# A decoder trunk on one core: three instead of two of eight pairs of a W_up group with seven products, 2048-column splits, token sums made late in the group

## The chip, the cores and the metric

The kernel runs on one core of a Trainium2 chip. The metric is the device time of one execution in microseconds. Five engines have their own in-order instruction queues and meet at semaphores: TensorE (PE, with its weight loads PEld), VectorE (DVE), ScalarE (ACT), GpSimd (POOL, nearly unused here) and SyncE (SP), which issues the DMAs.

## The reference

Two decoder layers over 256 tokens of width 2048, in float32. A layer has attention (sliding window in layer 0, block-sparse in layer 1, which for 256 tokens is causal attention; both with four memory heads), an output projection, a norm, and an MLP of width 8192. The change touches the MLP:

```python
mix = jnp.concatenate([self_out, mem_out], axis=-1) @ w_o[layer]
h = layer_norm(ALPHA * h + mix, ln_g[layer, 0], ln_b[layer, 0])
ffn = jnp.square(jax.nn.relu(h @ w_up[layer])) @ w_down[layer]
h = layer_norm(ALPHA * h + ffn, ln_g[layer, 1], ln_b[layer, 1])
```

## The kernel before, in words

**Products.** Every float32 operand is split into a high part (`hi`, rounded to the matmul's format by ScalarE, L96) and a low part (`lo`, the rest, by VectorE, L97). A product of a 128-row block of activations with a 512-column block of weights is three matmuls (L254 to L256): hi by hi, hi by lo, lo by hi. Each of the three first needs its weights' `hi` or `lo`.

**The MLP's order.** A layer's MLP is four chunks of 2048 hidden columns. A chunk has two W_up groups of 1024 columns, called its first and second UP group, and then two W_down groups, its first and second DOWN group. In layer 1 the first UP group of the first chunk, and in both layers the second DOWN group of the last chunk, are made by another function (`aform`, two half groups). So `mlp_group` makes 8 + 7 UP groups and 7 + 7 DOWN groups.

**A group.** `mlp_group` takes 16 blocks of 128 rows as eight pairs, in the order `ORDER`. A pair's weights are one DMA of 1 MB. Six pairs are normal: eight products, 24 matmuls, into the four PSUM banks `ps_g` (two token halves by two column halves). Two pairs (`FAST`, at places 2 and 4 of the order, counted from 0) take seven products, 21 matmuls. For these VectorE makes sums of weight blocks (`t`, L116, L119, L120) and, once for a set of activations, sums of token blocks (`fast_acts`, lines 125 to 137, into `sum_h` or `sum_g`). Four of the seven products go to four more banks `P1`, `P5`, `P6`, `P7`, which `early` (L486 to L490 in UP groups, L502 to L512 in DOWN groups) adds up after the last seven-product pair. At a group's end four VectorE instructions (L639 in UP groups) add the banks `ps_g` to these sums, and the banks are free for the next group.

**Between the groups.** Hooks in a group's first two pairs transpose the group before (`transposed`, L426 to L429: TensorE, then ScalarE, then VectorE) into `gT`, the DOWN groups' activations. `fast_acts(gt[0], sum_g)` is called in the hook of the second UP group's second pair, after the third of four transposes.

**Buffers and queues.** `raw` has 4 buffers of 2048 columns: DMA targets, the weight sums `t`, and `fast_acts`' workspace `x_f` take them in turn. `whi` and `wlo` have 7 buffers each of 1024 columns. `ps_mm` (for `ps_g`) and `ps_at` (for the four `P` banks and the transposes) have 4 banks each. A scheduler that runs before the kernel moves instructions of an engine past each other where nothing depends on the order, from its own estimate of when operands are ready; the built order is fixed.

Of the kernel before, what the change touches and what calls it, by code (L numbers as in the profile page):

```python
# [74 lines left out]
def trunk(ctx: ExitStack, tc: tile.TileContext, a: dict, out: bass.AP):  # L75
# [48 lines left out]
    def fast_acts(x, s_):  # L124


        raw = wp.tile([P, 2048], F32, name="x_f", tag="raw", bufs=NRAW)
        f = raw[:, :1024].rearrange("p (k t) -> p k t", k=4)
        nc.vector.tensor_tensor(f, x[:, :, 0].bitcast(F32), x[:, :, 1].bitcast(F32), ALU.add)
        a11, a21 = f[:, 0:4:2, :P], f[:, 0:4:2, P:]  # L130
        a12, a22 = f[:, 1:4:2, :P], f[:, 1:4:2, P:]
        s = raw[:, 1024:].rearrange("p (q u t) -> p q u t", q=4, u=2)
        nc.vector.scalar_tensor_tensor(s[:, 0], a21, -1.0, a22, op0=ALU.mult, op1=ALU.subtract)
        nc.vector.scalar_tensor_tensor(s[:, 1], s[:, 0], -1.0, a11, op0=ALU.mult, op1=ALU.subtract)
        nc.vector.tensor_tensor(s[:, 2], a11, a21, ALU.subtract)
        nc.vector.tensor_tensor(s[:, 3], a12, s[:, 1], ALU.subtract)
        split(s_[:, 0], s_[:, 1], raw[:, 1024:])
# [442 lines left out]
    for l in range(LAYERS):  # L580
# [148 lines left out]
```

## Time and profile before

| | us |
|---|---|
| median of 3 runs | 2082.78 (2081.52 to 2083.8) |
| the profiled execution | 2085.73, of which the trace's span is 2083.6 |
| TensorE busy | 2023.7 (97%) |
| VectorE busy | 1540.2 (74%) |
| ScalarE busy | 1045.6 (50%) |
| mean granted TensorE clock | 0.984 of full speed |

The profile is one execution. Busy time of TensorE says that matmuls are under way, not at which clock: the granted clock stands beside it in the views by window. A timeline row gives the start, the duration, the instruction and, in brackets, how long its engine was idle before it and what ended that.

### The profile page before, as it was taken

What the parts mean: (1) busy time and instruction counts of PE and PEld (TensorE: products, weight loads), DVE (VectorE), ACT (ScalarE), POOL (GpSimd) and SP (SyncE); (2) the same over time, 40 slices, a digit from 0 to 9 for tenths busy, and PEclk for the clock granted to TensorE, in tenths of its full rate; (3) what the DMA queues carried; (4) which work ended last, traced back from release to release, by engine and by line L of the source; (5) the groups of instructions that cost most, each with busy time, mean ns of one, the idle gap of its engine ahead of it and who ended that gap; (6) DMA issues with size and microseconds to landing.
All of it is one profiled execution on the core that took longest, in us unless ns stands there. A gap on an engine that the chain in (4) does not pass through costs nothing.

```text
span 2083.6 us, 23980 instructions
## 1 busy us (share of the span) xinstructions
PE 2023.7 (97%) x9326; PEld 1675.4 (80%) x9326; DVE 1540.2 (74%) x1951; ACT 1045.6 (50%) x1351; POOL 1.2 (0%) x8
## 2 busy tenths in 40 slices
PE   9999999999999999999999999999999999999997
PEld 7888888788778878878888888778887887888786
DVE  6566669688597868768885665769786876877785
ACT  5555535554464455456444554346445544654551
POOL 0000000000000000000000000000000000000000
PEclk9999999999999999999999999999999999999999
DMA  9644545455356545445754445425654554564562
GB/s 330 255 143 160 202 162 203 160 204 181 142 208 220 197 157 205 175 146 219 271 222 171 153 162 202 142 103 211 221 194 161 203 177 146 214 219 173 205 220 81
DMA packets 56273, 391.63 MB, mean 188 GB/s; under 512 B 6368, under 2 KB 6368, under 8 KB 9696
## 3 DMA queue, kind: packets, MB, share of 16 engines
q1 hardware_dynamic: 56160, 390.10, 52.1%
q8 instruction: 73, 1.20, 0.2%
q14 instruction: 40, 0.33, 0.0%
HBM read 387.98 MB, written 2.10 MB: 187 GB/s over the span
## 4 chain that ended last, share of the span: by engine, by line
PE 92%; DVE 6%; ACT 1%; issue 0%; DMA 0%; SPq 0%; DVEq 0%; ACTq 0%
PE ps_g L256 17%; PE ps_g L255 17%; PE ps_g L254 17%; PE ps_w L189 7%; PE ps_a L211 5%; PE ps_a L212 5%; PE ps_a L213 5%; PE ps_w L191 4%; PE P L254 3%; PE P L256 3%; PE P L255 3%; PE pt_h L426 2%; PE ps_m L536 1%; PE ps_m L538 1%; PE ps_m L537 1%; DVE h L419 1%
## 5 line engine op out<-in xcount | busy, mean ns | idle before, releaser
L97 DVE TENSOR_TENSOR wlo<-raw,whi 128x1024 fp32r<-128x1024 f32 (+1 forms) x706 | 815.7, 1174 | 329.0 <-ACT whi L96 324.9
L96 ACT CAST whi<-raw 128x1024 fp32r<-128x1024 f32 (+1 forms) x706 | 693.5, 1014 | 596.3 <-PE ps_g L256 323.6
L255 PE MATMUL ps_g<-wlo,hT 128*128 128x512 f32 x780 | 305.8, 392 | 0.1
L256 PE MATMUL ps_g<-whi,hT 128*128 128x512 f32 x780 | 305.9, 392 | 0.0
L254 PE MATMUL ps_g<-whi,hT 128*128 128x512 f32 x780 | 302.6, 395 | 0.9 <-ACT whi L96 0.7
L254 PE MATMUL ps_g<-whi,gT 128*128 128x512 f32 x728 | 285.3, 393 | 0.0
L256 PE MATMUL ps_g<-whi,gT 128*128 128x512 f32 x728 | 283.5, 390 | 0.0
L255 PE MATMUL ps_g<-wlo,gT 128*128 128x512 f32 x728 | 283.4, 390 | 0.0
L96 ACT CAST whi<-t 128x1024 fp32r<-128x1024 f32 x116 | 122.0, 1052 | 120.9 <-PE ps_g L256 45.0
L254 PEld LDWEIGHTS ps_g<-whi,hT 128*128 128x128 f32 x780 | 147.8, 190 | 33.7 <-ACT whi L96 3.8
L255 PEld LDWEIGHTS ps_g<-wlo,hT 128*128 128x128 f32 x780 | 147.7, 189 | 31.3 <-DVE wlo L97 0.5
L256 PEld LDWEIGHTS ps_g<-whi,hT 128*128 128x128 f32 x780 | 147.6, 189 | 31.0
L97 DVE TENSOR_TENSOR wlo<-t,whi 128x1024 fp32r<-128x1024 f32 x116 | 141.6, 1223 | 41.2 <-ACT whi L96 40.9
L256 PEld LDWEIGHTS ps_g<-whi,gT 128*128 128x128 f32 x728 | 136.7, 188 | 28.8
L255 PEld LDWEIGHTS ps_g<-wlo,gT 128*128 128x128 f32 x728 | 136.8, 188 | 27.6
L254 PEld LDWEIGHTS ps_g<-whi,gT 128*128 128x128 f32 x728 | 136.6, 188 | 27.2
L189 PE MATMUL ps_w<-hT,whi 128*128 128x512 f32 x320 | 119.9, 414 | 0.0
L189 PE MATMUL ps_w<-xT,whi 128*128 128x512 f32 x320 | 119.9, 414 | 0.0
L211 PE MATMUL ps_a<-whi,ot 128*128 128x512 f32 x256 | 101.7, 397 | 0.0
L213 PE MATMUL ps_a<-whi,ot 128*128 128x512 f32 x256 | 99.8, 390 | 0.0
L212 PE MATMUL ps_a<-wlo,ot 128*128 128x512 f32 x256 | 99.7, 389 | 0.0
L429 DVE TENSOR_TENSOR gT<-pt_h,gT 128x512 fp32r<-128x512 f32 x64 | 43.9, 688 | 67.0 <-ACT gT L428 67.0
(184 smaller groups left out, 2910.1 us busy)
## 6 DMA issues: line engine op xcount, KB each, us to landing
raw<-in_wup_dram SPq DMA_DIRECT2D x120, 1024.0 KB, 4.9
raw<-in_wdn_dram SPq DMA_DIRECT2D x112, 1024.0 KB, 4.9
raw<-in_wo_dram SPq DMA_DIRECT2D x32, 1024.0 KB, 4.8
raw<-in_wq_dram SPq DMA_DIRECT2D x24, 1024.0 KB, 4.8
raw<-in_wdn_s_dram SPq DMA_DIRECT2D x16, 1024.0 KB, 4.9
raw<-in_wmk_dram SPq DMA_DIRECT2D x8, 1024.0 KB, 6.2
raw<-in_wv_dram SPq DMA_DIRECT2D x8, 1024.0 KB, 7.3
raw<-in_wk_dram SPq DMA_DIRECT2D x8, 1024.0 KB, 4.8
```

The costliest lines, as they stand in the source:

```text
L96: nc.scalar.copy(hi, src)
L97: nc.vector.tensor_tensor(lo, src, hi.bitcast(F32), ALU.subtract)
L189: nc.tensor.matmul(ps, hi[:, kk:kk + P], x.rearrange("p s t -> p (s t)"), start=(k == 0), stop=False)
L191: nc.tensor.matmul(ps[:, :T], lo[:, kk:kk + P], x[:, 0], start=False, stop=(k == KT - 1))
L211: nc.tensor.matmul(ps[t], xh, hi, start=st, stop=False)
L212: nc.tensor.matmul(ps[t], xh, lo, start=False, stop=False)
L213: nc.tensor.matmul(ps[t], xl, hi, start=False, stop=en)
L254: nc.tensor.matmul(bank, xh, hi, start=st, stop=False)
L255: nc.tensor.matmul(bank, xh, lo, start=False, stop=False)
L256: nc.tensor.matmul(bank, xl, hi, start=False, stop=en)
L426: nc.tensor.transpose(pt[:, k], src[:, k * P:(k + 1) * P], ident)
L429: nc.vector.tensor_tensor(xt[:, :, 1, t * P:(t + 1) * P], pt, hi.bitcast(F32), ALU.subtract)
```

## The change

The numbers of a group become arguments. UP groups use `UP`: the order (3, 4, 0, 5, 1, 6, 2, 7) with pairs 0, 1 and 2 as seven-product pairs, at places 2, 4 and 6; `early` now comes after place 6. DOWN groups use `DOWN`, the numbers of before.

Weights are split 2048 columns at a time (1536 and 2048 in a seven-product pair: B11, B22, B21 and then the four sums); `whi` and `wlo` have 4 buffers each of 2048 columns. So that the three unchanged blocks lie side by side, the host stores a pair's last two blocks in the other order.

`fast_acts` is a generator of two steps, one for the sums and one for their split. For `sum_h` (three pairs now) the steps are in hooks of the first UP group's places 0 and 1; for `sum_g` in hooks of the second UP group's places 5 and 6. The sums have no buffers of their own for `sum_g`: they use those of `v` and `mk` of the attention, and `sum_h` uses `pts` for its third pair.

```diff
-NHI = 7
+NHI = 4
...
-ORDER = (2, 3, 0, 4, 1, 5, 6, 7)
-FAST = (0, 1)
+
+UP = ((3, 4, 0, 5, 1, 6, 2, 7), 3)
+DOWN = ((2, 3, 0, 4, 1, 5, 6, 7), 2)
...
-        def pair(s, n):
-            hi = wp.tile([P, 1024], F32R, name="whi", tag="whi", bufs=NHI)
-            lo = wp.tile([P, 1024], F32R, name="wlo", tag="wlo", bufs=NHI)
+        def pairs(s, n):
+            hi = wp.tile([P, 2048], F32R, name="whi", tag="whi", bufs=NHI)
+            lo = wp.tile([P, 2048], F32R, name="wlo", tag="wlo", bufs=NHI)
             split(hi[:, :n], lo[:, :n], s)
...
-        pair(raw[:, :1024], 1024)
-        nc.vector.tensor_tensor(t_[:, 0:2], b[:, 0:2], b[:, 2:3].broadcast_to([P, 2, 512]), ALU.subtract)
-        pair(b[:, 3], 512)
-        pair(t_[:, 0:2].rearrange("p q c -> p (q c)"), 1024)
+        pairs(raw[:, :1536], 1536)
+        nc.vector.tensor_tensor(t_[:, 0:2], b[:, 0:2], b[:, 3:4].broadcast_to([P, 2, 512]), ALU.subtract)
         nc.vector.tensor_tensor(t_[:, 2], b[:, 1], t_[:, 0], ALU.add)
-        nc.vector.tensor_tensor(t_[:, 3], b[:, 3], t_[:, 2], ALU.subtract)
-        pair(t_[:, 2:4].rearrange("p q c -> p (q c)"), 1024)
+        nc.vector.tensor_tensor(t_[:, 3], b[:, 2], t_[:, 2], ALU.subtract)
+        pairs(t_.rearrange("p q c -> p (q c)"), 2048)
...
+    def fast_acts(xs, units):
...
+        for j in range(0, len(units), 2):
+            n = len(units[j:j + 2])
+            x = xs[j // 2][:, :2 * n]
+            raw = wp.tile([P, 2, 8, P], F32, name="x_f", tag="raw", bufs=NRAW)
...
+            nc.vector.tensor_tensor(f, x[:, :, 0].bitcast(F32), x[:, :, 1].bitcast(F32), ALU.add)
...
+            nc.vector.scalar_tensor_tensor(s[:, :, 0], a21, -1.0, a22, op0=ALU.mult, op1=ALU.subtract)
+            nc.vector.scalar_tensor_tensor(s[:, :, 1], s[:, :, 0], -1.0, a11, op0=ALU.mult, op1=ALU.subtract)
+            nc.vector.tensor_tensor(s[:, :, 2], a11, a21, ALU.subtract)
+            nc.vector.tensor_tensor(s[:, :, 3], a12, s[:, :, 1], ALU.subtract)
+            parts += [s[:, u] for u in range(n)]
+        yield
+        for (hi, lo), s in zip(units, parts):
+            split(hi, lo, s)
+        yield
...
     def weights(src, parts=1):
...
+        hi = wp.tile([P, 2048], F32R, name="whi", tag="whi", bufs=NHI)
+        lo = wp.tile([P, 2048], F32R, name="wlo", tag="wlo", bufs=NHI)
+        for c in range(0, 2048, n):
+            split(hi[:, c:c + n], lo[:, c:c + n], raw[:, c:c + n])
+        return [(hi[:, c:c + 1024], lo[:, c:c + 1024]) for c in (0, 1024)]
...
                     if sum_h is None:
-                        sum_h = ap_.tile([P, 2, 4, 2, P], F32R, name="sum_h", tag="sum_h")
-                        fast_acts(hT[0], sum_h)
+                        sum_h = sum_units(UP[1], ("sum_h0", "sum_h1", "pts"))
+                        steps = fast_acts(hT, sum_h)
+                        hooks[0, 0] = hooks[1, 1] = lambda s=steps: next(s)
+                    if v_ == 1:
+                        steps = fast_acts(gt, sum_g)
+                        hooks[5, 0] = hooks[6, 0] = lambda s=steps: next(s)
...
                     transposed(us[b], gt[2 * v_ + b % 2], b // 2, 0)
-                    if v_ == 0 and b == 2:
-                        fast_acts(gt[0], sum_g)
```

**Place one: VectorE, first part of layer 0's third chunk's second UP group.** Before, its queue has the first group's transposed tiles (`gT`), the token sums (`x_f`, `sum_g`) and only then the weights of the seven-product pair at place 2 (`raw_5964`):

```order
L429 TENSOR_TENSOR gT0_5528<-pt_h_5884,gT0_5528 128x4x128
L429 TENSOR_TENSOR gT1_5529<-pt_h_5907,gT1_5529 128x4x128
L429 TENSOR_TENSOR gT0_5528<-pt_h_5926,gT0_5528 128x4x128
L129 TENSOR_TENSOR x_f_5933<-gT0_5528 128x1024
L429 TENSOR_TENSOR gT1_5529<-pt_h_5947,gT1_5529 128x4x128
L133 SCALAR_TENSOR_TENSOR x_f_5933<-x_f_5933 128x256
L135 TENSOR_TENSOR x_f_5933<-x_f_5933 128x256
L134 SCALAR_TENSOR_TENSOR x_f_5933<-x_f_5933 128x256
L136 TENSOR_TENSOR x_f_5933<-x_f_5933 128x256
L97 TENSOR_TENSOR sum_g_5532<-x_f_5933,sum_g_5532 128x1024
L116 TENSOR_TENSOR t_5966<-raw_5964 128x1024
L97 TENSOR_TENSOR wlo_5968<-raw_5964,whi_5967 128x1024
```

Now, in the same place, that pair's weights (`raw_5431`) and even the sums for the pair at place 4 (`t_5498`) stand ahead of or among the transposed tiles:

```order
L98 TENSOR_TENSOR wlo_5435<-raw_5431,whi_5434 128x1536
L654 TENSOR_TENSOR u_n_5286<-u_n_5286,ps_g_5053 128x512
L654 TENSOR_TENSOR u_n_5287<-u_n_5287,ps_g_5054 128x512
L118 TENSOR_TENSOR t_5433<-raw_5431,t_5433 128x512
L119 TENSOR_TENSOR t_5433<-raw_5431,t_5433 128x512
L117 TENSOR_TENSOR t_5498<-raw_5496 128x1024
L440 TENSOR_TENSOR gT0_5045<-pt_h_5363,gT0_5045 128x4x128
L118 TENSOR_TENSOR t_5498<-raw_5496,t_5498 128x512
L119 TENSOR_TENSOR t_5498<-raw_5496,t_5498 128x512
L98 TENSOR_TENSOR wlo_5442<-t_5433,whi_5441 128x2048
L440 TENSOR_TENSOR gT1_5046<-pt_h_5382,gT1_5046 128x4x128
L440 TENSOR_TENSOR gT0_5045<-pt_h_5401,gT0_5045 128x4x128
```

The token sums are gone from this place; the first pair's `lo` of 1536 columns stands before the end of the group before.

**Place two: VectorE, the end of the first UP group of that chunk.** Before, the sums of `early` lie among splits of the group's last pairs and of the next group's place 0, and the four additions of `ps_g` follow each other:

```order
L97 TENSOR_TENSOR wlo_5813<-raw_5806,whi_5812 128x1024
L488 TENSOR_TENSOR u_n_5730<-u_n_5731,P5_5606 128x512
L97 TENSOR_TENSOR wlo_5859<-raw_5856,whi_5858 128x1024
L489 TENSOR_TENSOR u_n_5731<-u_n_5731,P7_5608 128x512
L490 TENSOR_TENSOR u_n_5732<-u_n_5731,P5_5606 128x512
L97 TENSOR_TENSOR wlo_5863<-raw_5856,whi_5862 128x1024
L97 TENSOR_TENSOR wlo_5900<-raw_5897,whi_5899 128x1024
L97 TENSOR_TENSOR wlo_5904<-raw_5897,whi_5903 128x1024
L639 TENSOR_TENSOR u_n_5729<-u_n_5729,ps_g_5533 128x512
L639 TENSOR_TENSOR u_n_5730<-u_n_5730,ps_g_5534 128x512
L639 TENSOR_TENSOR u_n_5731<-u_n_5731,ps_g_5535 128x512
L639 TENSOR_TENSOR u_n_5732<-u_n_5732,ps_g_5536 128x512
```

Now `early` starts after the splits of the group's last pair and the next group's first, and its sums, the additions of `ps_g` and the next group's splits (`raw_5376` is its place 1, `raw_5431` its place 2) alternate:

```order
L117 TENSOR_TENSOR t_5433<-raw_5431 128x1024
L98 TENSOR_TENSOR wlo_5342<-raw_5339,whi_5341 128x2048
L498 TENSOR_TENSOR u_n_5286<-u_n_5284,P6_5117 128x512
L98 TENSOR_TENSOR wlo_5379<-raw_5376,whi_5378 128x2048
L499 TENSOR_TENSOR u_n_5285<-u_n_5286,P5_5116 128x512
L654 TENSOR_TENSOR u_n_5284<-u_n_5284,ps_g_5051 128x512
L500 TENSOR_TENSOR u_n_5286<-u_n_5286,P7_5118 128x512
L654 TENSOR_TENSOR u_n_5285<-u_n_5285,ps_g_5052 128x512
L501 TENSOR_TENSOR u_n_5287<-u_n_5286,P5_5116 128x512
L98 TENSOR_TENSOR wlo_5435<-raw_5431,whi_5434 128x1536
L654 TENSOR_TENSOR u_n_5286<-u_n_5286,ps_g_5053 128x512
L654 TENSOR_TENSOR u_n_5287<-u_n_5287,ps_g_5054 128x512
```

What frees the banks `ps_g` has moved behind two splits for the next group.

**Place three: VectorE, later in the second UP group.** Now the token sums stand here, among the weights of places 4 to 6 (`raw_5531` is place 5, `raw_5571` place 6):

```order
L133 TENSOR_TENSOR x_f_5537<-gT0_5045 128x1024
L98 TENSOR_TENSOR wlo_5507<-t_5498,whi_5506 128x2048
L137 SCALAR_TENSOR_TENSOR x_f_5537<-x_f_5537 128x2x128
L98 TENSOR_TENSOR wlo_5534<-raw_5531,whi_5533 128x2048
L138 SCALAR_TENSOR_TENSOR x_f_5537<-x_f_5537 128x2x128
L139 TENSOR_TENSOR x_f_5537<-x_f_5537 128x2x128
L140 TENSOR_TENSOR x_f_5537<-x_f_5537 128x2x128
L117 TENSOR_TENSOR t_5573<-raw_5571 128x1024
L118 TENSOR_TENSOR t_5573<-raw_5571,t_5573 128x512
L98 TENSOR_TENSOR wlo_5575<-raw_5571,whi_5574 128x1536
L98 TENSOR_TENSOR sums_5049<-x_f_5537,sums_5049 128x512
L98 TENSOR_TENSOR sums_5050<-x_f_5537,sums_5050 128x512
```

The sums of the weights for place 6 stand between the token sums and their split.

## Rows read from the trace of the kernel before

**Rows 1.** The page of the whole kernel: span, busy time, chain that ended last.
```profile
span 2083.6 us, 23980 instructions
...
PE 2023.7 (97%) x9326; PEld 1675.4 (80%) x9326; DVE 1540.2 (74%) x1951; ACT 1045.6 (50%) x1351; POOL 1.2 (0%) x8
...
PE 92%; DVE 6%; ACT 1%; issue 0%; DMA 0%; SPq 0%; DVEq 0%; ACTq 0%
```

**Rows 2.** Waits of the whole kernel: waiter <- releaser, total us, times, longest.
```profile
PE P L254 <- ACT whi L96: 38.3, 16, 3.5
```

**Rows 3.** Layer 0, third chunk: window, width, busy PE, PEld, DVE, ACT, POOL; PEclk, DMA.
```profile
694.20:736.40 42.20, 42.20 (x187) 34.93 (x187) 29.04 (x31) 21.34 (x25) 0.00 (x0) 1.00 0.50 177
736.40:788.90 52.50, 47.68 (x203) 38.18 (x202) 39.40 (x45) 28.25 (x36) 0.00 (x0) 0.93 0.49 177
788.90:833.10 44.20, 44.20 (x204) 36.56 (x203) 39.18 (x45) 24.55 (x30) 0.00 (x0) 1.00 0.55 193
833.10:875.20 42.10, 42.10 (x188) 34.86 (x187) 34.34 (x39) 19.80 (x22) 0.00 (x0) 1.00 0.56 200
752.60:761.20 8.60, 7.00 (x17) 5.00 (x18) 7.46 (x9) 4.48 (x6) 0.00 (x0) 0.61 0.34 122
```

**Rows 4.** TensorE's timeline in that stall: start us, us, instruction, [idle before <- releaser].
```profile
752.90 0.49 PE L254 MATMUL P<-whi,hT 128*128 128x512 f32 x1 [3.52 <-ACT whi L96]
...
755.42 0.79 PE L254 MATMUL P<-whi,sum_h 128*128 128x512 f32 x1 [1.27 <-ACT whi L96]
...
756.44 0.63 PE L256 MATMUL P<-whi,hT 128*128 128x512 f32 x1
756.87 0.63 PE L255 MATMUL ps_g<-wlo,hT 128*128 128x512 f32 x1
```

**Rows 5.** VectorE's timeline in that group, from the transposes' halves to the weights.
```profile
746.81 0.69 DVE L429 TENSOR_TENSOR gT<-pt_h,gT 128x512 fp32r<-128x512 f32 x1 [2.52 <-ACT gT L428]
747.53 1.23 DVE L129 TENSOR_TENSOR x_f<-gT 128x1024 f32<-128x1024 f32 x1
748.67 0.68 DVE L429 TENSOR_TENSOR gT<-pt_h,gT 128x512 fp32r<-128x512 f32 x1
749.27 0.42 DVE L133 SCALAR_TENSOR_TENSOR x_f<-x_f 128x256 f32<-128x256 f32 x1
...
751.93 1.23 DVE L97 TENSOR_TENSOR sum_g<-x_f,sum_g 128x1024 fp32r<-128x1024 f32 x1 [1.11 <-ACT sum_g L96]
753.07 1.22 DVE L116 TENSOR_TENSOR t<-raw 128x1024 f32<-128x1024 f32 x1
754.21 1.82 DVE L97 TENSOR_TENSOR wlo<-raw,whi 128x1024 fp32r<-128x1024 f32 x2
...
759.60 1.23 DVE L97 TENSOR_TENSOR wlo<-t,whi 128x1024 fp32r<-128x1024 f32 x1 [1.11 <-ACT whi L96]
760.75 3.49 DVE L97 TENSOR_TENSOR wlo<-raw,whi 128x1024 fp32r<-128x1024 f32 x3
```

**Rows 6.** Groups by form, VectorE and then ScalarE: line, op, shape, count, busy, mean.
```profile
L97 DVE TENSOR_TENSOR wlo<-raw,whi 128x1024 fp32r<-128x1024 f32 x644 | 776.0, 1221 | 326.9 <-ACT whi L96 322.8
...
L97 DVE TENSOR_TENSOR wlo<-raw,whi 128x512 fp32r<-128x512 f32 x62 | 42.3, 686 | 2.0 <-ACT whi L96 2.0
...
L96 ACT CAST whi<-raw 128x1024 fp32r<-128x1024 f32 x644 | 657.1, 1052 | 552.4 <-PE ps_g L256 282.4 <-PE ps_a L213 156.2 <-PE ps_w L189 63.0
...
L96 ACT CAST whi<-raw 128x512 fp32r<-128x512 f32 x62 | 38.4, 620 | 43.9 <-PE ps_g L256 41.2 <-DMA raw<-in_wmv_dram 2.1
```

**Rows 7.** Line 104, the load of a seven-product pair's weights.
```profile
DMA to landing us min/median/max: 4.6/4.9/7.2
```

**Rows 8.** TensorE's timeline at other idle stretches: layer 0's first group, layer 1's norm.
```profile
333.19 0.96 PE L254 MATMUL ps_g<-whi,hT 128*128 128x512 f32 x3 [0.70 <-ACT whi L96]
...
1336.58 1.32 PE L426 MATMUL pt_h<-ident,h 128*128 128x128 f32 x8 [2.04 <-DVE h L420]
...
1351.87 1.29 PE L426 MATMUL pt_h<-ident,h 128*128 128x128 f32 x8 [1.64 <-DVE h L420]
```

More of the change, by code (lines that the diff above doesn't have):

```diff
@@ L122, in fast_weights @@
+        pairs(t_.rearrange("p q c -> p (q c)"), 2048)
         return dict(zip(("B11", "B22", "B21", "T1", "T3", "T2", "T4"), tiles))
[L124 to L137, printed above, removed]
+    def fast_acts(xs, units):
+        parts = []
+        for j in range(0, len(units), 2):
+            n = len(units[j:j + 2])
+            x = xs[j // 2][:, :2 * n]
+            raw = wp.tile([P, 2, 8, P], F32, name="x_f", tag="raw", bufs=NRAW)
+            f = raw[:, 0, :4 * n].rearrange("p (k t) c -> p k (t c)", t=2)
+            nc.vector.tensor_tensor(f, x[:, :, 0].bitcast(F32), x[:, :, 1].bitcast(F32), ALU.add)
+            a11, a21 = f[:, 0:2 * n:2, :P], f[:, 0:2 * n:2, P:]
+            a12, a22 = f[:, 1:2 * n:2, :P], f[:, 1:2 * n:2, P:]
+            s = raw[:, 1, :4 * n].rearrange("p (u q) c -> p u q c", q=4)
+            nc.vector.scalar_tensor_tensor(s[:, :, 0], a21, -1.0, a22, op0=ALU.mult, op1=ALU.subtract)
[7 more added lines that the diff above has]
+        yield
@@ L139, in weights, with sum_units @@
+    def sum_units(n, tags):
+        units = []
+        for tag in tags[:n]:
+            if tag == "pts":
+                units.append([ap_.tile([P, 4, P], F32R, name="sums", tag="pts", bufs=2) for _ in range(2)])
+            else:
+                t_ = ap_.tile([P, 2, 4, P], F32R, name="sums", tag=tag)
+                units.append([t_[:, s] for s in range(2)])
+        return units
     def weights(src, parts=1):
@@ L233, in aform, with mlp_group @@
         return ps, finish
-    def mlp_group(src, xts, sums, hooks, early):
+    def mlp_group(src, xts, sums, hooks, early, order, nfast):
         ps = [ps_mm.tile([P, 512], F32, name="ps_g", tag="mm") for _ in range(4)]
@@ L242, in mlp_group @@
         last = {}
-        plan = []
-        for u in ORDER:
-            plan.extend([(u, b) for b in range(4)] if u not in FAST else [(u, i) for i in range(7)])
         fast = ("P1", 0, 1, "P5", "P7", "P6", 2)
-        for u in ORDER:
-            for i in range(7 if u in FAST else 4):
-                last[fast[i] if u in FAST else i] = (u, i)
+        for u in order:
+            for i in range(7 if u < nfast else 4):
+                last[fast[i] if u < nfast else i] = (u, i)
         def mm3(bank, x, w, st, en):
@@ L259, in tok @@
             return [xts[k // 4][:, k % 4, s, t * P:(t + 1) * P] for s in range(2)]
-        left = len([u for u in ORDER if u in FAST])
-        for pos, u in enumerate(ORDER):
+        left = nfast
+        for pos, u in enumerate(order):
             k0, k1 = 2 * u, 2 * u + 1
-            if u in FAST:
+            if u < nfast:
                 for i in range(4):
@@ L270, in mlp_group @@
                 w = fast_weights(src[u])
-                sx = [[sums[:, s, q, u % 2] for s in range(2)] for q in range(4)]
+                sx = [[s[:, q] for s in sums[u]] for q in range(4)]
                 prods = (("P1", tok(k0, 0), "B11"), (0, tok(k1, 0), "B21"), (1, sx[3], "B22"),
@@ L617, in trunk @@
             todo = []
-            sum_g = ap_.tile([P, 2, 4, 2, P], F32R, name="sum_g", tag="sum_g")
+            sum_g = sum_units(DOWN[1], ("v", "mk"))
             for v_ in range(CH // 1024):
@@ L642, in trunk, with back @@
                     us = acc
-                def back(b, v_=v_, us=us, gt=gt, sum_g=sum_g):
+                def back(b, v_=v_, us=us, gt=gt):
                     transposed(us[b], gt[2 * v_ + b % 2], b // 2, 0)
-                    if v_ == 0 and b == 2:
-                        fast_acts(gt[0], sum_g)
                 todo = [lambda b=b, f=back: f(b) for b in (0, 1, 2, 3)]
```

17 lines of the change are left out of this document (4 added, 13 removed).

## The prediction, as it was put on record

> **What bounds the kernel now.** I read the page first. TensorE is busy for 97% of the span and holds 92% of the chain that ended last [rows 1]: the end moves only by matmuls that go or by TensorE's waits. The list of waits came next. One stands out: matmuls into the `P` banks wait for ScalarE's `whi` 16 times, 3.5 us at the longest [rows 2]. The reader is to see in the timeline that they come in pairs, 3.52 and then 1.27 us [rows 4], so there are eight such stalls; the second UP group of every chunk has one, at its first seven-product pair (layer 1's first chunk too, there its only `mlp_group` UP group).
>
> The windows by group price a stall. A second UP group and the first DOWN group after it had the same 186 matmuls and 16 transposes, and took 52.5 and 44.2 us [rows 3]: a stall costs 8.3 us. [...] Transposes cost 44.2 - 42.1 = 2.1 us a group [rows 3].
>
> The cause is in VectorE's timeline. The third transposed tile comes at 746.81, the token sums run from 747.53 to the end of `sum_g`'s `lo` at 753.16, and only behind them come the seven-product pair's weight sums (753.07) and `lo` parts (754.21, 759.60) [rows 5]. ScalarE's casts queue behind `sum_g`'s cast in the same way, so TensorE has no weights at 749.4 and starts at 752.90 [rows 4].
>
> **The change part by part.** Durations: a VectorE split of 1024 columns takes 1.221 us and one of 512 takes 0.686 [rows 6], so 512 columns more are 0.535 us. Back to back, starts are closer than durations: three splits of 1024 in 3.49 us are (3.49 - 1.22) / 2 = 1.135 apart, and 512 columns 0.60 (748.67 to 749.27) [rows 5]. Estimates from these: 1536 columns 1.67, 2048 columns 2.2 us. ScalarE's cast of 2048 is 1.052 + 2 x 0.432 = 1.92 us [rows 6].
>
> *Fewer matmuls.* 8 + 7 UP groups lose three matmuls each: 45 x 0.227 = -10.2 us, all on the path.
>
> *The stalls.* In the built order the splits and sums of the pair at place 2 now stand ahead of the transposed tiles or among them (place one). I followed that queue from the group's start, 0. VectorE has the next pair's four weight sums split at 9.4 to 10; TensorE wants them at 14.6 (two normal pairs 10.9, transposes 1.7, nine matmuls 2.0). The split for place 3 is done at 13.2 and wanted at 17.4, that for place 4 at 15.9 and wanted at 22.8, its sums at 19.2 and wanted at 24.8. The token sums run from 15.9 on, their split ends at 27.5, and they are not wanted before the DOWN group. The weight sums for place 6 are split at 32.3, wanted at 35.1: the closest, 2.8 us. So all eight stalls go: 8 x 8.3 = -66.4 us. If one stays, 8.3 us stay.
>
> *What is late next, the end of a UP group.* `early` now comes after place 6, with one normal pair left instead of three. From the end of product `P6` until TensorE needs the third bank `ps_g` of the next group there are 3 + 24 + 12 matmuls, 8.8 us. VectorE has in that time (place two) seven instructions of 512 columns as far as the third bank's addition, six at 0.60 and the last at 0.69 (4.3), a split of 2048 and one of 1536 (3.9): 8.2 us. So nothing is lost if VectorE is at L498 when `P6` ends, and whatever it is later is lost but for 0.6, of which the matmul's own latency takes some. In the second UP group it is there in time by my count (37.5 against 37.5). In the first UP group the sum L117 for the next group's place 2 stands in front (place two); its `raw` buffer comes free when place 6's sums are split (27.6), the load takes 4.9 us [rows 7], and the queue behind it reaches L498 at 36.1, 0.3 to 0.5 after `P6`. With a load of 7.2 us [rows 7] it would be 2.8. Behind L117 wait the split for the next place 0, `early` and the bank additions, and for those TensorE. I take 0.8 us for each of the six later chunks with such a group, +5 us; bounds 0 and 6 x 2.8 = 17.
>
> *VectorE's load.* A second UP group has 8 splits of 2048, 3 of 1536, 3 sums of 1024, 20 instructions of 512, and the token sums' 1.14 + 4 x 0.33: 17.6 + 5.0 + 3.4 + 12.0 + 2.5 = 40.5 us, against 183 x 0.227 + 2.1 = 43.6 us of TensorE. The first has 34.5 against 41.5. It fits, with 3 us of air in the tightest group.
>
> [...]
>
> *The first chunk of layer 0.* Its built order was made with VectorE late: three pairs' token sums instead of two come between the norm and the first weights (two more sums, four short ones and a split of 512, some 2.5 us), and there was a wait of 0.70 us there before [rows 8]. In its second UP group the sums for place 2 stand behind the transposed tiles, and each seven-product pair's split waits for ScalarE's cast of the sums made just before it. My count gives VectorE 1 to 2.2 us late at seven such places and less at three, some 10 us in the chunk. I take +10; bounds 0 (the count starts too late) and 16 (the clock falls twice as well).
>
> *Wider splits elsewhere.* In the norms a split that stands between steps of the chain takes 2.2 instead of 1.135 us. TensorE already waits 2.04 and 1.64 us in layer 1's norm [rows 8]. I take 1 us in each of three norms, +3; bounds 0 and 7 (a longer stretch at the lower clock behind the wait of 2.04). In the attention and W_o stages TensorE did not wait for splits, and 4 buffers of 2048 hold more than 7 of 1024 did; I cost it at nothing, and 1.1 us a place if that cover goes.
>
> Sum on the profiled execution's own time: 2085.73 - 10.2 - 66.4 + 5 + 10 + 3 = 2027.1 us. The median of the runs is 2.95 lower: **2024 us**.
>
> **The rivals.**
>
> *All of it and nothing new.* Speaks for it: the load of 40.5 us in 43.6. Against: the margin of a few tenths at each UP group's end. 2082.8 - 76.6 = 2006 us.
>
> *VectorE becomes the bound in the UP groups.* It is 43.9 us by durations, and it also idles some 4 us in a second UP group (2 before the first transposed tile, 2 for the cast of place 6's sums): 47.9 against 43.6, 4.3 us in each of eight, and 2.1 in each of seven first ones. 34 + 15 + 3 on top of 2006: 2058 us. Against it: in the old second UP group VectorE worked 39.4 us by durations in 52.5 [rows 3] and caught up.
>
> *Slower: the banks come late at every UP group.* Place: the additions that free `ps_g`, behind two splits for the next group. The idle wait of 2.04 us was enough for matmuls at the lower clock in layer 1, that of 1.64 was not [rows 8]. If VectorE is 3 us late at L498, TensorE idles 2.4 to 2.7 us, and a stretch of 12 matmuls at 0.43 [rows 4] instead of 0.227 adds 2.4: some 5 us at each of 15 groups, about the 76.6 in all, no gain. From a little over 3 us on it is slower; at 4 us, 2006 + 15 x 6.1 = 2098. For it: L117's wait for its load. Against: that is one group in two, and my count has it 0.5 late.
>
> [...] The idle of 1.64 us and that of 0.70 [rows 8] brought no such stretch here, so I leave its chance small.
>
> **How the numbers follow.** Likeliest 0.68 (its own range 2012 to 2042), all of it 0.13, VectorE bound 0.15, slower 0.04. A difference under 0.2% (4 us) can't be told from none here. Faster 0.95, same 0.01, slower 0.04. The range of 8 in 10 is 2006 to 2048: down to the first rival, whose floor is firm, since nothing else is removed, and up past the bounds of the single costs (17, 16 and 7, where the likeliest has 5, 10 and 3) to where the second rival begins.
>
> **What would show it.** Right: no pair of waits of a `P` matmul for `whi` in the second UP groups, windows of them at 43.6 to 45 us with a granted clock of 1.00, first UP groups at 41.5 to 43, the token sums' `lo` done long before the DOWN group. TensorE's short waits then stand at the third bank `ps_g` of a group, released by L654, and in layer 0's first chunk. Wrong: second UP groups over 47 us, VectorE busy without a gap through them, a granted clock under 1 at the groups' starts, or waits of the `P` matmuls moved to places 4 or 6.

## The result, and the profile after

The changed kernel takes 2019.47 us (median of 4 runs, 2018.94 to 2022.86), the kernel before 2082.6 (4 runs): ratio 0.970, interval 0.9683 to 0.9717. Forecast were 2024 us and a range of 2006 to 2048. The profiled execution took 2018.94 us, 66.8 less than that of before.

The page of the changed kernel, the same three lines as in [rows 1]:

```profile
span 2017.2 us, 22882 instructions
...
PE 1991.5 (99%) x9281; PEld 1652.1 (82%) x9281; DVE 1565.4 (78%) x1626; ACT 1011.2 (50%) x971; POOL 1.2 (0%) x8
...
PE 90%; DVE 4%; ACT 2%; issue 1%; DMA 1%; SPq 0%; DVEq 0%; ACTq 0%
```

TensorE's busy time fell by 32 us, though 45 matmuls are only 10. The rest goes with the clock: the mean granted clock of the span rose from 0.984 to 0.996, since matmuls behind the stalls no longer run at the lower clock (0.61 in the window of a stall [rows 3], where the same group now has 1.00, below).

TensorE's waits (waiter <- releaser, total us, times, longest):

```profile
PE pt_h L437 <- DVE h L431: 3.2, 1, 3.2
PE ps_g L265 <- ACT whi L97: 2.7, 7, 0.6
PE pt_h L437 <- ACT u_n L656: 2.1, 2, 1.2
...
PE P L265 <- ACT whi L97: 1.1, 1, 1.1
PE ps_g L265 <- DVE u_n L654: 0.8, 2, 0.4
```

The 16 waits of [rows 2] have become one of 1.1 us. The banks at the UP groups' ends, where the prediction put 5 us, cost two waits of 0.4.

The windows that answer to [rows 3], layer 0's third chunk, group by group (same columns):

```profile
678.76:720.30 41.54, 41.54 (x185) 34.41 (x184) 32.43 (x25) 21.67 (x15) 0.00 (x0) 1.00 0.54 190
720.30:764.00 43.70, 43.70 (x202) 36.10 (x201) 40.52 (x40) 28.17 (x28) 0.00 (x0) 1.00 0.54 196
764.00:807.70 43.70, 43.70 (x202) 36.17 (x201) 39.51 (x36) 23.49 (x20) 0.00 (x0) 1.00 0.55 201
807.70:849.90 42.20, 42.20 (x188) 34.96 (x187) 33.72 (x29) 18.67 (x11) 0.00 (x0) 1.00 0.55 200
```

The second UP group went from 52.50 to 43.70 us at a granted clock of 1.00; VectorE works 40.52 us in it, and the prediction had counted 40.5. The DOWN groups, which the change leaves alone, are as they were.

VectorE's timeline in that second UP group shows the token sums in their new place:

```profile
743.36 1.22 DVE L117 TENSOR_TENSOR t<-raw 128x1024 f32<-128x1024 f32 x1
...
746.89 1.29 DVE L98 TENSOR_TENSOR sums<-x_f,sums 128x512 fp32r<-128x512 f32 x2
748.09 0.69 DVE L119 TENSOR_TENSOR t<-raw,t 128x512 f32<-128x512 f32 x1
750.84 2.29 DVE L98 TENSOR_TENSOR wlo<-t,whi 128x2048 fp32r<-128x2048 f32 x1 [2.05 <-ACT whi L97]
```

They end at 748.2, 16 us before the DOWN group that uses them.

Where the 66.4 us of span came from, read as the starts of the stages' first matmuls in the two traces (the rows add up to the difference of the spans but for rounding):

| stretch | before | after | difference |
|---|---|---|---|
| start to layer 0's first W_k product | 77.0 | 74.8 | -2.2 |
| layer 0: attention, W_o, norm | 254.1 | 255.7 | +1.6 |
| layer 0, first chunk: UP, DOWN | 96.0, 86.2 | 90.4, 86.7 | -5.6, +0.5 |
| layer 0, second and third: UP pairs, DOWN pairs | 94.6 and 94.7, 86.2 and 86.3 | 84.9 and 84.9, 86.3 and 86.2 | -19.5, 0 |
| layer 0, fourth: UP | 94.6 | 85.0 | -9.6 |
| layer 0's last DOWN groups to layer 1's first W_k product | 136.1 | 139.7 | +3.6 |
| layer 1: attention, W_o, norm, first half groups | 282.7 | 284.2 | +1.6 |
| layer 1, first chunk: UP group | 52.4 | 43.4 | -9.1 |
| layer 1, second to fourth: UP pairs | 94.6, 94.6, 94.7 | 85.6, 85.6, 84.9 | -27.8 |
| layer 1: DOWN groups to the end | 86.2, 86.3, 86.2, 100.0 | 86.2, 86.2, 86.3, 100.1 | +0.2 |

An UP pair without trouble is 84.9 us. The change pays in full there; some 10 us are missing elsewhere, and the experiments look for these.

### The profile page after: what moved, and what is told of

Same layout as the page of the kernel before. It is cut to its first block, busy times and chain, and to the rows that moved or that the text cites. A ratio compares the mean times of both kernels' runs of the same rounds, so it can differ in the third digit from the quotient of the medians.

```text
span 2017.2 us, 22882 instructions
## 1 busy us (share of the span) xinstructions
PE 1991.5 (99%) x9281; PEld 1652.1 (82%) x9281; DVE 1565.4 (78%) x1626; ACT 1011.2 (50%) x971; POOL 1.2 (0%) x8
## 3 DMA queue, kind: packets, MB, share of 16 engines
q1 hardware_dynamic: 56160, 390.10, 53.7%
## 4 chain that ended last, share of the span: by engine, by line
PE 90%; DVE 4%; ACT 2%; issue 1%; DMA 1%; SPq 0%; DVEq 0%; ACTq 0%
PE ps_g L265 15%; PE ps_g L267 15%; PE ps_g L266 15%; PE ps_w L203 7%; PE ps_a L226 6%; PE ps_a L225 6%; PE ps_a L227 6%; PE ps_w L205 4%; PE P L266 3%; PE P L267 3%; PE P L265 3%; DVE wlo L98 2%; PE pt_h L437 2%; ACT whi L97 2%; PE ps_m L547 1%
## 5 line engine op out<-in xcount | busy, mean ns | idle before, releaser
L98 DVE TENSOR_TENSOR wlo<-raw,whi 128x2048 fp32r<-128x2048 f32 (+2 forms) x357 | 766.6, 2149 | 285.2 <-ACT whi L97 284.3
L97 ACT CAST whi<-raw 128x2048 fp32r<-128x2048 f32 (+2 forms) x357 | 641.6, 1802 | 562.5 <-PE ps_g L267 269.6
L265 PE MATMUL ps_g<-whi,hT 128*128 128x512 f32 x690 | 271.0, 395 | 2.7 <-ACT whi L97 1.9
L266 PE MATMUL ps_g<-wlo,hT 128*128 128x512 f32 x690 | 268.9, 390 | 0.0
L267 PE MATMUL ps_g<-whi,hT 128*128 128x512 f32 x690 | 268.8, 390 | 0.0
L97 ACT CAST whi<-t 128x2048 fp32r<-128x2048 f32 x73 | 139.6, 1912 | 163.8 <-DVE t L119 146.9
L98 DVE TENSOR_TENSOR wlo<-t,whi 128x2048 fp32r<-128x2048 f32 x73 | 167.2, 2291 | 64.6 <-ACT whi L97 63.6
L266 PEld LDWEIGHTS ps_g<-wlo,gT 128*128 128x128 f32 x728 | 136.8, 188 | 27.7 <-DVE wlo L98 0.2
L265 PEld LDWEIGHTS ps_g<-whi,hT 128*128 128x128 f32 x690 | 129.3, 188 | 31.2 <-ACT whi L97 4.0
L267 PEld LDWEIGHTS ps_g<-whi,hT 128*128 128x128 f32 x690 | 129.6, 188 | 27.3
L266 PEld LDWEIGHTS ps_g<-wlo,hT 128*128 128x128 f32 x690 | 129.7, 188 | 26.3 <-DVE wlo L98 0.3
L117 DVE TENSOR_TENSOR t<-raw 128x1024 f32<-128x1024 f32 x73 | 89.1, 1221 | 18.5 <-DMA raw<-in_wup_dram 17.9
```

The costliest lines, as they stand in the source:

```text
L117: nc.vector.tensor_tensor(t_[:, 0:2], b[:, 0:2], b[:, 3:4].broadcast_to([P, 2, 512]), ALU.subtract)
L265: nc.tensor.matmul(bank, xh, hi, start=st, stop=False)
L266: nc.tensor.matmul(bank, xh, lo, start=False, stop=False)
L267: nc.tensor.matmul(bank, xl, hi, start=False, stop=en)
```

## The experiments

All ratios are against runs of the kernel before on the same chip. They were made on three chips, on which the kernel before had medians between 2082.47 and 2083.89 us; the intervals of the ratios reach some 2.7 us to either side.

**The late sums alone (e1).** The kernel before, with the token sums for the DOWN groups moved to places 5 and 6 of the second UP group (`fast_acts` in two steps, as in the change); two pairs, 1024-column splits.

```diff
+                    if v_ == 1:
+                        steps = fast_acts(gt[0], sum_g)
+                        hooks[5, 0] = hooks[6, 0] = lambda s=steps: next(s)
...
-                    if v_ == 0 and b == 2:
-                        fast_acts(gt[0], sum_g)
```

> The kernel before with one part of the change: the token sums of the DOWN groups are made in the second UP group's places 5 and 6. Two seven-product pairs and splits of 1024 columns stay. My theory (eight stalls of 8.3 us go because the token sums no longer stand ahead of the first seven-product pair's weights): 2082.6 - 66.4 = 2016 us, up to 2022 with small waits; no pair of waits of 3.5 and 1.3 us of a P matmul in the second UP groups. Rival (the wide splits shorten the chain and do the most of it): over 2050 us.

Measured: 2016.1 us, ratio 0.9674 (0.9661 to 0.9687). No wait of a `P` matmul for `whi` is left in its list, and the second UP group of layer 0's third chunk takes 43.70 us at a granted clock of 1.00:

```profile
719.40:763.10 43.70, 43.70 (x202) 36.20 (x201) 38.34 (x44) 27.07 (x34) 0.00 (x0) 1.00 0.52 190
```

Those few lines are worth the predicted eight stalls, and do no worse than the whole change.

**The change without late sums (e2).** The token sums back in the hook of the third transpose.

```diff
-                    if v_ == 1:
-                        steps = fast_acts(gt, sum_g)
-                        hooks[5, 0] = hooks[6, 0] = lambda s=steps: next(s)
...
+                    if v_ == 0 and b == 2:
+                        for _ in fast_acts(gt, sum_g):
+                            pass
```

> The changed kernel with the token sums back in the second UP group's second pair, behind the third transposed tile; three seven-product pairs and splits of 2048 stay. My theory: the stalls come back, 8 x 8.3 = 66 us or more (the weights' chain has wider steps, and the clock falls again): 2080 to 2095 us. Rival (third pair and wide splits carry the gain): under 2040 us.

Measured: 2098.78 us, ratio 1.0074 (1.0062 to 1.0087): slower than before, and some 4 us above the range of the theory. TensorE's longest waits, and the window of the second UP group of layer 0's third chunk:

```profile
PE P L265 <- ACT whi L97: 32.2, 8, 4.0
PE P L266 <- DVE wlo L98: 12.2, 9, 2.0
```

```profile
737.60:791.30 53.70, 47.42 (x201) 36.84 (x200) 39.09 (x39) 28.05 (x26) 0.00 (x0) 0.94 0.41 152
```

The eight stalls are back, each now 53.7 - 43.7 = 10.0 us; 8 x 10.0 is, within a microsecond, the difference from the changed kernel. The stall is dearer than the 8.3 us of before; its two waits in TensorE's timeline are 4.02 and 1.56 us, where [rows 4] has 3.52 and 1.27, and the second is now for `lo`:

```profile
754.55 0.56 PE L265 MATMUL P<-whi,hT 128*128 128x512 f32 x1 [4.02 <-ACT whi L97]
...
757.51 0.80 PE L266 MATMUL P<-wlo,hT 128*128 128x512 f32 x1 [1.56 <-DVE wlo L98]
```

**Two pairs (e3) and narrow splits (e4).** With e1 these two fill a table of two by two. Its corners are not quite clean: e1 is built from the kernel before, so it also lacks the new order of a pair's blocks and makes `sum_h` in one step.

```diff
-UP = ((3, 4, 0, 5, 1, 6, 2, 7), 3)
+UP = ((2, 3, 0, 4, 1, 5, 6, 7), 2)
```

> The changed kernel with two seven-product pairs in the UP groups, in the order of before; late token sums and wide splits stay. My theory: 45 matmuls of 0.227 us come back (+10.2), the waits in layer 0's first chunk (4.6 us in the changed kernel's trace) go for the most part: 2019.5 + 10.2 - 4 = 2026 us, 2023 to 2030. Rival (the third pair costs on VectorE what it saves on TensorE): 2019 or less.

```diff
-NHI = 4
+NHI = 7
...
+            for c0 in range(0, n, 1024):
+                m = min(1024, n - c0)
+                hi = wp.tile([P, 1024], F32R, name="whi", tag="whi", bufs=NHI)
+                lo = wp.tile([P, 1024], F32R, name="wlo", tag="wlo", bufs=NHI)
+                split(hi[:, :m], lo[:, :m], s[:, c0:c0 + m])
```

> The changed kernel with splits of 1024 columns and 7 buffers as before; third pair and late token sums stay. By the spacing of back-to-back instructions a second UP group has 8 x 0.07 + 3 x 0.07 = 0.8 us more work on VectorE, 41.3 of 43.7 us: no change beyond a few us, 2017 to 2026 us. Rival (the whole fixed part of an instruction is exposed, 11 x 0.15 = 1.6 us a group, and VectorE becomes the bound of the second UP groups): 2030 us or more, with waits in every second UP group.

| late sums, and | two pairs | three pairs |
|---|---|---|
| 1024-column splits | 2016.1, 0.9674 (0.9661 to 0.9687) | 2007.35, 0.9633 (0.962 to 0.9646) |
| 2048-column splits | 2019.07, 0.969 (0.9677 to 0.9703) | 2019.47, 0.970 (0.9683 to 0.9717) |

Both theories were missed; e3 came to the number of its rival. The third pair brings 8.7 us with narrow splits and nothing with wide ones; wide splits cost 12 us with three pairs and 3 with two. The traces show where: in the steady chunks wide splits cost nothing (an UP pair takes 84.9 us with three seven-product pairs and 86.3 with two, wide or narrow; the 85.6 of two UP pairs of layer 1 aside). With two pairs the 3 us are mostly in the attention, 1.5 in each layer. Most of the rest needs both: layer 0's first UP pair takes 87.6 us wide with two pairs (e3), 87.7 narrow with two (e1), 85.2 narrow with three (e4) and 90.4 with both. Narrow splits and three pairs reach the time of the prediction's rival "all of it and nothing new", 2006.

**Which part of the wide split (e10, e11, e12).** First the buffers of 2048 stay, and only the instructions become narrow:

```diff
-            split(hi[:, :n], lo[:, :n], s)
+            for c in range(0, n, 1024):
+                m = min(n, c + 1024)
+                split(hi[:, c:m], lo[:, c:m], s[:, c:m])
...
+        n = min(n, 1024)
         for c in range(0, 2048, n):
```

> The changed kernel with its 4 weight buffers of 2048 columns, but every split made as instructions of at most 1024 columns. It tells apart why the narrow version of the changed kernel (1024-column instructions and 7 buffers of 1024) was 12 us faster. Theory A, length of the instruction: a 2048-column split holds its in-order queue for 2.29 us (VectorE) or 1.91 us (ScalarE), and what stands behind it, or waits for its first half, is that much late; then this run comes at 2006 to 2010 us. Theory B, the buffers: a buffer of 2048 columns comes free only when both halves have been used, so the next cast starts later; then this run stays at 2016 to 2021 us. I hold A likelier, since in layer 0's first chunk the waits of the changed kernel are ScalarE's casts waiting for VectorE's sums, not for buffers.

Measured: 2004.65 us, ratio 0.9627 (0.9614 to 0.964), just below the range of theory A. The length of the instruction is the whole cost; the buffers cost nothing (against e4 the intervals overlap). Then one engine at a time:

```diff
     def split(hi, lo, src):
-        nc.scalar.copy(hi, src)
-        nc.vector.tensor_tensor(lo, src, hi.bitcast(F32), ALU.subtract)
+        nc.scalar.copy(hi, src)
...
+        for c in range(0, n, 1024):
+            m = min(n, c + 1024)
+            nc.vector.tensor_tensor(lo[:, c:m], src[:, c:m], hi[:, c:m].bitcast(F32), ALU.subtract)
```

> The changed kernel, with ScalarE's casts still 2048 (1536) columns at a time and VectorE's splits in instructions of 1024 at most. With the next run it tells whose wide instruction costs the 14.8 us between the changed kernel (2019.5) and the same buffers with narrow instructions (2004.65). Theory: the dependency, since the first half of `lo` can't start before the whole cast is through; then the wide cast alone keeps most of the loss: 2011 to 2018 us. Rival: VectorE's queue, held for 2.29 us by one split, is what counts, and this run comes back to 2004 to 2010 us.

In e12 the loop stands around ScalarE's copy instead.

> The changed kernel, with ScalarE's casts in instructions of 1024 at most and VectorE's splits still 2048 (1536) columns at a time: the other half of the comparison. Theory (the wide cast costs most): 2006 to 2013 us. Rival (VectorE's queue): 2012 to 2019 us.

Measured: wide casts 2012.45 us, ratio 0.9661 (0.9648 to 0.9674); wide splits of VectorE 2006.39, ratio 0.9632 (0.9619 to 0.9645). The cast costs most, as expected: 7.8 us alone, VectorE's split 1.7 alone (within what can be told from none), and the two together 14.8, so some 5 us come only from both. Stretches in the traces show where:

| us | both narrow (e10) | VectorE wide (e12) | ScalarE wide (e11) | both wide (changed kernel) |
|---|---|---|---|---|
| layer 0: attention, W_o, norm | 254.0 | 254.1 | 254.9 | 255.7 |
| layer 0, first chunk's UP pair | 85.0 | 85.5 | 89.8 | 90.4 |
| layer 0's last DOWN groups to layer 1's first W_k product | 136.8 | 137.1 | 137.4 | 139.7 |
| layer 1: attention, W_o, norm, half groups | 282.1 | 282.1 | 282.0 | 284.2 |

With three pairs, the first chunk's loss is ScalarE's, but for half a microsecond. ScalarE's timeline in the changed kernel, at the second UP group's place 6, then VectorE's and TensorE's:

```profile
409.19 0.59 ACT L497 COPY u_n<-P 128x512 f32<-128x512 f32 x1 [5.79 <-PE P L267]
409.68 1.90 ACT L97 CAST whi<-t 128x2048 fp32r<-128x2048 f32 x1
```

```profile
408.31 0.69 DVE L119 TENSOR_TENSOR t<-raw,t 128x512 f32<-128x512 f32 x1
411.61 2.29 DVE L98 TENSOR_TENSOR wlo<-t,whi 128x2048 fp32r<-128x2048 f32 x1 [2.61 <-ACT whi L97]
```

```profile
411.63 0.97 PE L265 MATMUL P<-whi,sums 128*128 128x512 f32 x3 [1.12 <-ACT whi L97]
...
413.44 0.74 PE L265 MATMUL ps_g<-whi,hT 128*128 128x512 f32 x2 [0.60 <-ACT whi L97]
```

A 2048-column cast of the weight sums can start only when the last of the four sums (L119, 409.0) is made, and TensorE gets the first of them only when the whole cast is through, 411.6. In layer 0's first chunk, where the engines have no lead, both delays reach TensorE. With two pairs (e3) they do not, though its casts are as wide: the list of its first UP pair has one wait of TensorE, 0.4 us. Here the copy of `P1` (L497), which waits for TensorE, stands in front as well.

The wait in layer 1's norm is set by VectorE's split. The transposes' waits in the changed kernel, e12, e11 and e10 (one fence each):

```profile
1307.92 1.94 PE L437 MATMUL pt_h<-ident,h 128*128 128x128 f32 x8 [3.19 <-DVE h L431]
```

```profile
1297.41 1.94 PE L446 MATMUL pt_h<-ident,h 128*128 128x128 f32 x8 [3.18 <-DVE h L440]
```

```profile
1302.52 1.23 PE L446 MATMUL pt_h<-ident,h 128*128 128x128 f32 x8 [2.13 <-DVE h L440]
```

```profile
1294.62 1.23 PE L440 MATMUL pt_h<-ident,h 128*128 128x128 f32 x8 [2.13 <-DVE h L434]
```

3.2 us with VectorE's splits wide, 2.1 narrow; [rows 8] had 2.04. The stage as a whole moves only when both are wide, and most of what it then loses is not in the norm: from the first W_k product to the first of W_o, both layers' attention takes 136.9 us in the kernel before, in e10 and in e12, 137.5 and 136.8 in e11, and 138.4 and 138.3 in the changed kernel. TensorE's list has no wait there; the 1.5 us are spread over the heads in steps of 0.1 to 0.4 us.

**Early sums at the group's end (e5).** What the slower rival spoke of, built as a kernel: the last seven-product pair at place 7, so that `early` starts at the group's end.

```diff
-UP = ((3, 4, 0, 5, 1, 6, 2, 7), 3)
+UP = ((3, 4, 0, 5, 1, 6, 7, 2), 3)
```

> The changed kernel with the third seven-product pair of a UP group at the last place (7) instead of 6, so that the sums of `early` start only at the group's end. It produces what the slower rival of the prediction spoke of: the additions that free the banks `ps_g` come late at every one of 15 UP groups. Theory: from the end of P6 to the third bank's first matmul there are then some 15 matmuls (3.4 us) instead of 39 (8.8 us), against 8.2 us of VectorE's instructions: 4.8 us late at each group, more with a stretch at the lower clock behind it (up to 2.4 us): 2019 + 15 x 4.8 to 15 x 7.2, 2090 to 2127 us, slower than before. Rival: VectorE's order moves the bank additions ahead of the splits and most of the lateness is gone: 2025 to 2050 us.

Measured: 2086.88 us, ratio 1.0019 (1.001 to 1.0028), just under the range of the theory. TensorE's first wait, one of its 15 stalls, VectorE's queue before it, and the window behind:

```profile
PE ps_g L265 <- DVE u_n L654: 49.2, 15, 4.3
```

```profile
741.24 0.47 PE L265 MATMUL ps_g<-whi,hT 128*128 128x512 f32 x1 [3.13 <-DVE u_n L654]
```

```profile
735.34 2.29 DVE L98 TENSOR_TENSOR wlo<-raw,whi 128x2048 fp32r<-128x2048 f32 x1 [0.52 <-ACT whi L97]
737.55 0.68 DVE L498 TENSOR_TENSOR u_n<-u_n,P 128x512 f32<-128x512 f32 x1
738.15 1.75 DVE L98 TENSOR_TENSOR wlo<-raw,whi 128x1536 fp32r<-128x1536 f32 x1
739.82 0.68 DVE L499 TENSOR_TENSOR u_n<-u_n,P 128x512 f32<-128x512 f32 x1
740.41 0.68 DVE L654 TENSOR_TENSOR u_n<-u_n,ps_g 128x512 f32<-128x512 f32 x1
```

```profile
741.20:748.00 6.80, 6.76 (x27) 5.53 (x28) 6.17 (x8) 4.03 (x8) 0.00 (x0) 0.75 0.32 104
```

Behind every UP group the next one waits for the banks, 49.2 / 15 = 3.3 us, and pays (2085.4 - 2017.2) / 15 = 4.5 us with the lower clock behind it (0.75). The mechanism of the slower rival is real, at its place and near its price; one place in the order decides it.

**More seven-product pairs (e9, e13).** Three pairs in the DOWN groups, on top of e4; four in the UP groups, on top of e10. Both keep the extra token sums in buffers of the attention's `qt`.

```diff
-DOWN = ((2, 3, 0, 4, 1, 5, 6, 7), 2)
+DOWN = ((3, 4, 0, 5, 1, 6, 2, 7), 3)
```

> The narrow version of the changed kernel (2007 us), and three seven-product pairs in the W_down groups too: order (3, 4, 0, 5, 1, 6, 2, 7) there, token sums for the third pair. Gain: 14 groups x 3 matmuls x 0.227 = 9.5 us. Theory: the W_down groups' `early` (eight instructions of VectorE and their chain, some 10.5 us) doesn't fit in the 8.8 us left behind place 6, so each of 14 groups waits some 1.7 us: 2007 - 9.5 + 24 = 2021 us (2013 to 2030). Rival: it fits as in the UP groups: 1997 to 2000 us, the best version.

```diff
-UP = ((3, 4, 0, 5, 1, 6, 2, 7), 3)
+UP = ((4, 0, 5, 1, 6, 2, 3, 7), 4)
```

> The changed kernel with 1024-column instructions, and four instead of three seven-product pairs in a UP group: order (4, 0, 5, 1, 6, 2, 3, 7), token sums for the fourth pair. It tests the prediction's rival that VectorE becomes the bound of the UP groups. Gain: 15 x 3 x 0.227 = 10.2 us. Theory: a second UP group has then some 41 + 4 (weight sums 2.3, 1.7 of splits) = 45 us of VectorE against 43.0 of TensorE, so 2 us are lost in each of eight, 16 us, and more in layer 0's first chunk: 2010 to 2030 us, worse than three pairs. Rival: VectorE has room over the chunk as a whole: 1995 to 1998 us.

Measured: e9 2015.11 us, ratio 0.9674 (0.9661 to 0.9687), in the theory's range, but not by its mechanism: no wait for banks leads the list, but transposes that wait for the UP groups' results.

```profile
PE pt_h L458 <- ACT u_n L677: 5.3, 7, 1.7
```

In layer 0's third chunk the DOWN pair took 86.0 us, where e4 had 86.3 and three matmuls less in each group make 84.9, and the UP pair 85.8 instead of 84.9. The largest piece is at the end of layer 0's fourth UP pair, which takes 91.2 us instead of 84.9: waits of 1.67, 0.90 and 0.80 us in a row, with a granted clock of 0.76 in the 7 us from the first (933.40 to 940.40). How the rest divides was not followed; the profiled execution (2019.17 us) was also the slowest of the five.

e13: 2004.36 us, ratio 0.9621 (0.9608 to 0.9635), the same as three pairs (e10); both expectations missed. The second UP group of layer 0's third chunk:

```profile
715.10:757.80 42.70, 42.70 (x197) 35.28 (x196) 42.34 (x53) 28.86 (x37) 0.00 (x0) 1.00 0.50 186
```

VectorE works 42.34 of 42.70 us and still doesn't make TensorE wait: the UP pair takes 83.6 us, 1.3 less than e10's 84.9. What the fourth pair gains in the later chunks it loses in layer 0's first (89.1 us against 85.0) and in its last DOWN groups to layer 1 (139.3 against 136.8). The best versions are e10 and e13, about 15 us under the changed kernel.

## Why the prediction was right

The direction, the mechanism of the large term and the size held: 2019.47 against 2024 us. Of the change's three parts the late token sums alone bring the gain (e1, 2016.1 us); third pair and wide splits cancel each other. How close the total came is partly luck, since the errors of the small terms cancel: the banks, the first chunk and the norms were put 12 us too high together, and two stretches put at nothing cost 6.6. By the prediction's own terms, in the two profiled executions:

| term | predicted | measured | from |
|---|---|---|---|
| fewer matmuls | -10.2 | -10.5 | UP pair 84.9 against 86.3 with two pairs (e3), 7.5 pairs |
| eight stalls | -66.4 | -66.4 | 94.6 - 84.9 - 1.4 = 8.3 a pair; e1 shows it alone |
| banks at the UP groups' ends | +5 | +1.4 | two waits of 0.4; 85.6 instead of 84.9 in two pairs |
| layer 0's first chunk | +10 | +4.5 | -5.6 and +0.5, where an undisturbed chunk has -9.7 |
| wider splits, norms | +3 | +0.1 | layer 1's first norm with W_o and half groups, 129.2 to 129.3; layer 0's first norm and the one between the layers unchanged |
| wider splits, attention | 0 | +3.0 | 136.9 to 138.4 and 138.3 |
| layer 0's last DOWN groups | 0 | +3.6 | its first group takes 47.9 us instead of 44.2 |
| start | 0 | -2.2 | |

*Stalls.* The step that carries the number: the pair of waits, its cause in VectorE's queue and its price, 8.3 us. That is more than the 4.8 us of its two waits: behind them matmuls started 0.43 us apart [rows 4], where a group without a stall took 42.2 / 186 = 0.227 us for each [rows 3]. The window of these matmuls in the kernel before has a granted clock of 0.50:

```profile
756.40:761.20 4.80, 4.80 (x13) 3.69 (x12) 3.66 (x5) 2.67 (x3) 0.00 (x0) 0.50 0.19 80
```

e1 takes the cause away alone and e2 puts it back alone; both times the eight waits follow. The count of VectorE's queue held too: from the group's start the token sums' split ends at 27.9 us (counted 27.5) and that of place 6's weight sums at 33 (counted 32.3).

*Banks.* The sum L117 does wait for its load, as the prediction said (12 times, 3.3 us at most, 17.9 in all), but the lateness reached TensorE at two groups of 15 only (layer 1's second and third chunk). The bound of 17 was far off.

*Layer 0's first chunk.* The chunk was right, the size was half: six waits of TensorE, 3.0 us in all, the longest 1.12. I had not seen that it takes the wide cast as well as the third pair: with narrow instructions and three pairs (e10) the chunk loses nothing, with wide ones and two pairs (e3) no more than with narrow ones (e1). What in the third pair matters there was not taken apart.

*Norms and attention.* One wait in layer 1's norm grew by 1.15 us, close to the 1 taken, but the second one of [rows 8], 1.64 us, is gone, and the norms cost nothing in sum. "I cost it at nothing" failed for the attention stages, where the loss comes with both splits wide, with two pairs (e3) as with three. It also left out layer 0's last DOWN groups. There the changed kernel's transposes wait for ScalarE:

```profile
937.71 0.66 PE L437 MATMUL pt_h<-ident,u_n 128*128 128x128 f32 x4 [1.19 <-ACT u_n L656]
939.28 0.66 PE L437 MATMUL pt_h<-ident,u_n 128*128 128x128 f32 x4 [0.91 <-ACT u_n L656]
```

The wide splits are not the whole cause here. With wide splits and two pairs (e3) the group takes 44.1 us and has no such wait; with narrow splits and three pairs it takes 46.7 in e4, with waits of 0.9 us at the same place, and 45.0 in e10. So the loss comes with the third pair, and the wide splits add to it. In the changed kernel ScalarE's and VectorE's queues also have the casts and splits of `memt`, loaded for layer 1, at this place; whether these make the difference from the other chunks was not tested.

The start's -2.2 us was not predicted; in the other runs' traces the same stretch is between 74.7 and 76.5, and I did not look for the cause.

*The rivals.* "All of it and nothing new" is what e4 and e10 reach; what kept the change from it are the wide instructions, 15 us, for which the prediction had 3 (in the norms, where they cost nothing) and part of the first chunk's 10. "VectorE becomes the bound" fell: 40.52 us busy in 43.70, and with four pairs 42.34 in 42.70. Its 43.9 us were my estimate: the count of VectorE's load, with durations in place of spacings (2.291 us for 2048 columns, 1.756 for 1536, 1.22 for a sum of 1024, 0.686 for 512, and 1.23 + 4 x 0.42 for the token sums, from [rows 5, 6]). No run shows that durations add up so; the trace has the 40.52 us. Fewer and wider instructions did lower VectorE's own load (1565.4 us busy in the changed kernel, 1595.7 in e10) and not the time: e10 is the faster. "Banks late" did not occur in the change, and e5 shows it one place further on.

The profiled execution of before lies 2.95 us above its median and that of after 0.53 below: of the 8 us by which the profiled sum was too high, 3.5 are that, and the forecast was 4.5 us off.

## What to carry to other kernels

On an in-order queue, work that nobody needs soon must not stand ahead of work that somebody needs next: moving the token sums half a group later was worth 66 us without one instruction less. The wide instructions saved time of their engine (VectorE was busy for 1565.4 us, in e10 for 1595.7) but delayed the first half of their result: TensorE got it when the whole cast was through, after 1.90 us, where a cast of 1024 columns took 1.05 [rows 6]. They won nowhere: they cost nothing in the steady chunks, where the consumer has a lead, and 15 us in the other stretches. The saving showed only where that lead was kept (84.9 us for a steady UP pair, 90.4 for layer 0's first): look at the first and the last group of a stage, not only at the steady ones.

## What the runs showed of the hardware

In e5 and in the kernel before the stalls cost more than their idle time, and the length of a wait alone did not say how much. Waits of some 3.3 us in e5 cost 4.5 us each, with a granted clock of 0.75 in the 6.8 us from the first matmul; the stall of 3.52 and 1.27 us before cost 8.3, with 0.61 in its window [rows 3]. The wait of 3.19 us in layer 1's norm was followed by a granted clock of 0.55 in the changed kernel (first row) and of 1.00 in e2, where the same transposes waited 3.19 us too (second row; the column before the last two is the granted clock):

```profile
1307.90:1314.90 7.00, 6.98 (x26) 5.76 (x27) 6.16 (x8) 1.89 (x4) 0.00 (x0) 0.55 0.32 128
```

```profile
1346.70:1353.70 7.00, 6.90 (x37) 5.57 (x38) 6.90 (x11) 2.35 (x4) 0.00 (x0) 1.00 0.30 124
```

In e5 the granted clock was 0.58 to 0.76 in the 7 us behind each of the 15 waits, and between two of them it was back at 1.00 (748.10 to 789.40). In the kernel before it was 0.76 in the 7 us behind the wait of 2.04 us in layer 1's norm, and 1.00 behind those of 1.64 and 0.70 [rows 8]:

```profile
1336.50:1343.50 7.00, 6.90 (x30) 5.42 (x31) 6.13 (x10) 2.35 (x4) 0.00 (x0) 0.76 0.52 202
1351.80:1358.80 7.00, 6.88 (x35) 5.32 (x36) 5.76 (x9) 4.35 (x6) 0.00 (x0) 1.00 0.11 13
333.10:340.10 7.00, 6.91 (x30) 5.75 (x31) 6.93 (x7) 4.45 (x6) 0.00 (x0) 1.00 0.64 243
```

In the changed kernel's first UP pair of layer 0, with waits of up to 1.12 us, it was 1.00 over the whole pair:

```profile
330.50:420.90 90.40, 87.42 (x385) 69.68 (x384) 77.33 (x69) 51.34 (x46) 0.00 (x0) 1.00 0.53 188
```

In e13 VectorE was busy for 42.34 of the 42.70 us of a group, and TensorE for all of them. In the kernel before it was busy for 39.40 of 52.50 us [rows 3], and TensorE waited: the order of the queue decided, not the share.
